# A two-layer diffusion trunk on one core: output groups over four PSUM banks, splits without GpSimd, and modulation groups and gating matmuls in other places

## The chip, the cores and the metric

The kernel runs on one core of a Trainium2 chip. The metric is the device time of one execution in microseconds; a lower time is better. Several executions are timed and the median is given, and one further execution is profiled. The engines are TensorE (PE: matmuls, with weight loads listed apart as PEld), VectorE (DVE), ScalarE (ACT), GpSimd (POOL) and the sync engine (SP), which here only issues transfers.

## The reference, cut to what matters

The program computes one inference step of a two-layer network for 512 latent tokens and 128 context tokens, 640 token columns in all, of width 1024. A conditioning vector (`c` for latent tokens, `c_ctx` for context tokens) gives nine modulation vectors for each layer, and each layer has a half-step feed-forward block, a mixer and a second half-step feed-forward block:

```
mod = (silu(cond) @ ada_w[i] + ada_b[i])                 # 9 vectors of 1024
h = modulate(rms_norm(x, g0), mod[0], mod[1]); x += 0.5 * mod[2] * swiglu(h)
h = modulate(rms_norm(x, g1), mod[3], mod[4]); x += mod[5] * mixer(h)
h = modulate(rms_norm(x, g2), mod[6], mod[7]); x += 0.5 * mod[8] * swiglu(h)
swiglu(h) = (silu(h @ w_g) * (h @ w_u)) @ w_out          # inner width 2816
```

The mixer of layer 0 has retention heads beside a spatial gating part (`u * (w_s @ rms_norm(v) + b_s)`), the mixer of layer 1 is differential attention. All values are fp32.

## The kernel before, in words

Activations lie with features on the 128 partitions and the 640 tokens along the free axis, in two halves of 320 columns. Each weight and each activation is split into a high part rounded to fp32r and a low part with the rest, and a product is three matmuls (high by high, high by low, low by high: lines 695, 696 and 697, in `mm3x`), here called a step. `tick()` after each step moves every waiting generator on by one.

**Weights and splits.** One list, `order`, holds every weight group and every modulation group in the order of use. The sync engine issues the loads in that order (`emit_load`, `pump`) into two raw buffers of 1 MB, the ring; a load waits until a buffer is released. `split_piece` makes the high part on ScalarE (line 308, tile `whi`) and the low part on VectorE (line 309, `wlo`), or on GpSimd where it is called so: twice before the first matmuls and twice for the second group of the first block.

**Feed-forward blocks.** Each of the four blocks has 22 inner groups of 128 features, in three stages of 6, 8 and 8. The first two groups go as a pair (in the very first block by `first_wide`), the third plainly, and the rest by a Strassen scheme (`strassen_in`) with seven products into three PSUM tiles `pu`, `pg`, `pf`. Its last VectorE and ScalarE instructions make the high and low part (`a...h`, `a...l`) of the group's activation. After each stage, `out_proj` multiplies the stage's 6 or 8 activations by four output groups `fout` of two column blocks each. For a column block and a half, `op_step` takes one PSUM bank, runs over all activations in order, and VectorE adds the result to the residual (`x_update`, tile `xs`).

**Modulation groups.** There are 36 for each layer. One kind (`ada`) runs on TensorE: 16 matmuls in a row, ahead of a feed-forward group; four such groups share a PSUM bank until the fourth is done. The other kind (`ada_v`, the set `ADV`) runs on VectorE: four passes over the raw buffer with a dot product against conditioning rows `sb`, which `load_condb` loads (1 MB) and ScalarE puts through SiLU. `mid_ada` starts such a group within an output stage as soon as the list comes to it. `weave` puts VectorE groups behind output groups and TensorE groups ahead of the feed-forward groups in `FA`.

**Order on the engines.** Most instructions are placed by a planner that works from its own estimates; `high_priority` moves a traced instruction ahead. SP is in written order throughout; TensorE, VectorE and ScalarE are in written order at the start, and TensorE through the Strassen groups and output stages. In the mixer of layer 0 the gating part (`sgu`) yields `SGW` ticks after its norm before its matmuls `mx` are issued.

Of the kernel before, what the change touches and what calls it, by code (L numbers as in the profile page):

```python
# [11 lines left out]
F32R = mybir.dt.float32r  # L12
I32 = mybir.dt.int32
AF = mybir.ActivationFunctionType
# [4 lines left out]
P = 128  # L19
# [15 lines left out]
NG0 = 3  # L35
FA = (4, 6, 9, 12, 14, 18)
QD_ = 512
# [3 lines left out]
NPRE = 10  # L41
SGW = 11
FYO = (0, 3, 4, 1, 5, 6, 2, 7)
# [16 lines left out]
C_N = 1280  # L60
ADV = {(0, g) for g in range(12, 36)} | {(1, g) for g in range(24)}
PHASES = ((0, 0), (0, 1), (0, 2), (1, 0), (1, 1), (1, 2))
# [5 lines left out]
def trunk_kernel(  # L68
# [153 lines left out]

    def weave(ws, ads, pads=(), fins=()):
        r, ads, pads = [], list(ads), list(pads)
        for w in ws:
            if pads and w[0] == "fin" and w[3] in fins:
                r.append(pads.pop(0))
            r.append(w)
            if ads and w[0] != "fin" and not (w[0] == "ein" and w[1] < 2):
                r.append(ads.pop(0))  # L230
        assert not ads and not pads
        return r
# [4 lines left out]
    order = order[:2] + w00[:1] + order[2:q] + w00[1:2] + order[q:]  # L237
    l1, pl = ada_groups(1, range(6)), ada_groups(1, range(6, 9))
    order += weave(w00[2:], ada_groups(0, [3, 4, 5]), ada_groups(0, [2]), (2, 3, 4, 5))
    order += weave([("ein", g) for g in range(10)] + [("eout", g) for g in range(4)], ada_groups(0, [6, 7, 8]))  # L240
    order += weave(ffn_order(0, 1), l1[:12], pl[:6], FA)
    order += weave(ffn_order(1, 0), l1[12:], pl[6:], FA)
    order += [("oin", g) for g in OORD] + [("oout", c, g) for c in range(2) for g in range(2)]
# [29 lines left out]

    def split_piece(sub=V):
        while st["sp"] < nord and order[st["sp"]][0] == "ada":
            st["sp"] += 1
        j = st["sp"]
        if j >= nord:
# [19 lines left out]
        else:  # L298
            nq = 1
            n = wtab[key][1] // 2 * 256  # L300
            t = r[:, h * n:(h + 1) * n]
        hi = wp.tile([P, 1024], F32R, tag="whi", bufs=5, name=f"whi{j}_{h}")
        lo = wp.tile([P, 1024], F32R, tag="wlo", bufs=5, name=f"wlo{j}_{h}")
        if key[0] == "fin":
            hf, lf = (v[:, :nq * QD_].rearrange("p (q x) -> p q x", q=nq) for v in (hi, lo))
        else:
            hf, lf = hi[:, :n], lo[:, :n]
        S.activation(out=hf, in_=t, func=AF.Copy)  # L308
        sub.tensor_tensor(out=lf, in0=t, in1=hf.bitcast(F32), op=ALU.subtract)  # L309
# [395 lines left out]
    def first_wide(i, keys, names):  # L705
# [13 lines left out]
        for c in SQ:  # L719
            if c in "ab":  # L720
                gs.append(ada(order[st["i"]]))
                next(gs[-1])
            elif c == "T":
                for g in gs:
                    next(g)
            elif c == "F":
                for g in gs:
                    for _ in g:
                        pass
                gs = []  # L730
                apply_all2((n, n + 1))
                n += 2
            elif c == "W":
                W1 = next_group(keys[1])
                split_piece(nc.gpsimd)
                split_piece(nc.gpsimd)
            elif c == "G":
                assert kg < n
                go(0, kg, W0, (0, 1))
                kg += 1  # L740
            elif c == "g":
                assert kw < n
                go(1, kw, W1, (0,))
                kw += 1
        assert kg == kw == KD
        load_condb()
        sg.__exit__(None, None, None)
# [63 lines left out]
    def out_proj(keys, acts, l, gmod, nxt, ks=None):  # L811
        nw = len(keys) if nxt is None else 2
        for gi in range(nw):
            W = next_group(keys[gi])
            for j in range(2):
                for hf in range(2):
                    op_step(keys[gi], W, gi, j, hf, acts, l, gmod, nxt, ks)
                    mid_ada()
            W.done()
# [5 lines left out]
        for n_, hf in enumerate((1, 0) if end else (0, 1)):  # L825
# [9 lines left out]
            chains[nxt, hf] = spawn(norm_chain(nxt, hf, NW[hf]))  # L835

    def op_step(key, W, gi, j, hf, acts, l, gmod, nxt, ks):
        ps = psm("op" + "_".join(str(v) for v in key[1:]) + f"_{j}{hf}")
        mm_fm(ps, W, j, acts, hf, ks)
        if nxt is None:  # L840
            x_update(ps, 2 * gi + j, l, gmod, hf)
        else:
            with tc.high_priority(HP):
                x_update(ps, 2 * gi + j, l, gmod, hf)
                norm_acc(nxt, hf, 2 * gi + j)

# [46 lines left out]
    def ffn(i, l, s, nxt):  # L893
        base = 0
        for ci, n in enumerate(CHUNKS):
# [35 lines left out]
            for g in range(g0, base + n):  # L931
                e = start_g(g)
                strassen_in(i, l, s, g, e)
                acts.append(e[:2])
            lastf = nxt if ci == len(CHUNKS) - 1 else None
# [587 lines left out]
    for _ in rsqrt(r, m, 5, "n0"):  # L1523
        pass
    split_piece(nc.gpsimd)
    split_piece(nc.gpsimd)
    warm(WU[2])
# [6 lines left out]
    for hf, (t0, t1) in enumerate(HALVES):  # L1534
        bc = psm(f"n0b{hf}")
        PE.matmul(bc[:, :t1 - t0], ones, dg[:, t0:t1], start=True, stop=True)
        t = stmp(f"bcs{hf}")
        S.copy(out=t[:, :t1 - t0], in_=bc[:, :t1 - t0])
        bcs[0, hf] = t
        prod[0, hf] = 0  # L1540
# [10 lines left out]

    apply_all2((0, 1))
    tb[0] = spawn(tbuild(0))
# [114 lines left out]
```

## Time and profile before

| what | value |
|---|---|
| median of the timed runs (lowest to highest) | 2477.71 us (2469.72 to 2481.81) |
| the profiled execution's own time | 2478.16 us |
| span of its profile | 2476.1 us |
| mean granted TensorE clock | 0.987 |
| TensorE busy | 2395.3 us (97%) |
| VectorE busy | 1840.8 us (74%) |
| ScalarE busy | 1067.4 us (43%) |
| GpSimd busy | 63.7 us (3%) |

The span runs from the first to the last instruction of the profiled execution. Busy time is the time in which an engine had an instruction in work; TensorE's instructions overlap and their ends are modelled, so its share says when it had work and not how fast it went. The granted clock is the share of full speed at which TensorE was let run.

### The profile page before, as it was taken

To read this page: it belongs to the slowest core of one execution; us is meant where nothing else is said; L and a number is where in the kernel's file an instruction comes from. 1 tells how busy PE (TensorE), PEld (TensorE's weight loads), DVE (VectorE), ACT (ScalarE), POOL (GpSimd) and SP (SyncE) were. 2 spreads that over 40 slices of the span, in tenths; PEclk is the share of its full clock that TensorE was granted. 3 is DMA by queue.
4 is the path that set the end of the run, shared out by engine and by line. 5 is a ranking of instruction groups with operands and counts; after the bars stand their busy time and mean duration, and the time that the engine had idled before them with its cause. 6 is when DMAs were issued, how large, how long until landed. Compare 5 with 4: busy or idle time off the path is not lost.

```text
span 2476.1 us, 40714 instructions
## 1 busy us (share of the span) xinstructions
PE 2395.3 (97%) x16530; PEld 2342.1 (95%) x16530; DVE 1840.8 (74%) x3749; ACT 1067.4 (43%) x2018; POOL 63.7 (3%) x86
## 2 busy tenths in 40 slices
PE   8999999999899999999999999999999999999998
PEld 6899999899899999999999999999999989999998
DVE  7677867877878777677977776789788878574664
ACT  4525335333226335153542423536777646252442
POOL 1000000000000000000000000001011000000000
PEclk8999999999999999999999999999999999999999
DMA  7342423323231433423234242242111111222121
GB/s 277 112 151 86 154 71 115 137 105 124 79 136 69 137 120 119 153 96 124 91 108 145 96 175 89 103 171 74 42 43 57 54 35 67 81 87 91 69 103 43
DMA packets 44476, 259.30 MB, mean 105 GB/s; under 512 B 5889, under 2 KB 8577, under 8 KB 16769
## 3 DMA queue, kind: packets, MB, share of 16 engines
q1 hardware_dynamic: 41024, 252.37, 28.6%
q8 instruction: 129, 2.11, 0.4%
q0 software_dynamic: 1280, 2.62, 0.3%
q10 hardware_dynamic: 1984, 1.72, 0.2%
q14 instruction: 59, 0.48, 0.1%
HBM read 252.76 MB, written 3.93 MB: 104 GB/s over the span
## 4 chain that ended last, share of the span: by engine, by line
PE 80%; DVE 9%; DMA 4%; ACT 4%; issue 2%; POOL 0%; POOLq 0%; ACTq 0%; DVEq 0%
PE op L696 8%; PE op L697 8%; PE op L695 8%; PE pu L695 6%; PE pu L696 6%; PE pu L697 6%; PE pg L697 3%; DVE wlo L309 3%; PE pg L696 3%; PE pg L695 3%; PE pf L695 3%; PE pf L696 3%; PE pf L697 3%; ACT whi L308 2%; DMA raw<-in_w_fout 2%
## 5 line engine op out<-in xcount | busy, mean ns | idle before, releaser
L309 DVE TENSOR_TENSOR wlo<-raw,whi 128x1024 fp32r<-128x1024 f32 (+1 forms) x480 | 528.8, 1118 | 286.0 <-ACT whi L308 284.9
L308 ACT ACTIVATE whi<-raw 128x1024 fp32r<-128x1024 f32 (+1 forms) x484 | 465.0, 976 | 639.7 <-DMA raw<-in_w_fout 144.1
L807 DVE SCALAR_TENSOR_TENSOR xs<-op,mod,xs 128x128 f32<-128x128 f32 (+2 forms) x312 | 126.9, 435 | 135.1 <-PE op L697 134.6
L524 ACT ACTIVATE nq<-xs 128x320 f32<-128x320 f32 x84 | 39.0, 468 | 135.1 <-DVE xs L807 133.3
L406 DVE CUSTOM_DVE_ANT_0 raw<-raw,sb 128x1024 f32<-128x1024 f32 x72 | 87.4, 1218 | 0.7
L404 DVE SCALAR_TENSOR_TENSOR raw<-raw,sb 128x1024 f32<-128x1024 f32 x72 | 87.5, 1220 | 0.5
L695 PE MATMUL oq<-H4h,whi 128*128 128x320 f32 x256 | 81.1, 318 | 0.2 <-ACT ov L979 0.2
L697 PE MATMUL oq<-H4h,wlo 128*128 128x320 f32 x256 | 79.6, 311 | 0.0
L696 PE MATMUL oq<-H4l,whi 128*128 128x320 f32 x256 | 79.3, 310 | 0.0
L1316 DVE TENSOR_REDUCE amx<-as 128x1 f32<-128x320 f32 x144 | 61.5, 460 | 19.1 <-PE as L1312 18.8
L1324 ACT ACTIVATE ap<-as,anm 128x320 f32<-128x320 f32 x128 | 66.2, 531 | 14.1 <-DVE anm L1319 13.9
L696 PE MATMUL pf<-H5p,whi 128*128 128x320 f32 x172 | 53.8, 313 | 2.0 <-DVE H5p L614 2.0
L871 ACT COPY p<-pg 128x320 f32<-128x320 f32 x76 | 32.5, 427 | 53.8 <-PE pg L697 53.6
L696 PE MATMUL pf<-H3p,whi 128*128 128x320 f32 x172 | 53.5, 312 | 1.8 <-DVE H3p L614 1.8
L696 PE MATMUL pf<-H2p,whi 128*128 128x320 f32 x172 | 53.4, 312 | 1.8 <-DVE H2p L614 1.8
L695 PE MATMUL pf<-H0p,whi 128*128 128x320 f32 x172 | 54.3, 318 | 0.2 <-ACT H0p L609 0.2
L696 PE MATMUL pf<-H0p,whi 128*128 128x320 f32 x172 | 53.9, 313 | 0.2 <-DVE H0p L614 0.2
L695 PE MATMUL pf<-H5p,whi 128*128 128x320 f32 x172 | 53.9, 317 | 0.0
L695 PE MATMUL pf<-H3p,whi 128*128 128x320 f32 x172 | 53.8, 317 | 0.0
L695 PE MATMUL pf<-H2p,whi 128*128 128x320 f32 x172 | 53.8, 316 | 0.0
L291 DVE TENSOR_TENSOR raw<-raw 128x512 f32<-128x512 f32 x76 | 52.4, 689 | 1.9
L697 PE MATMUL pf<-H0p,wlo 128*128 128x320 f32 x172 | 53.8, 313 | 0.0
(2691 smaller groups left out, 8835.6 us busy)
## 6 DMA issues: line engine op xcount, KB each, us to landing
raw<-in_w_fin SPq DMA_DIRECT2D x88, 1024.0 KB, 4.7
raw<-in_ada_w SPq DMA_DIRECT2D x64, 1024.0 KB, 4.8
raw<-in_w_fout SPq DMA_DIRECT2D x32, 1024.0 KB, 4.7
raw<-in_w_fout SPq DMA_DIRECT2D x16, 768.0 KB, 4.1
raw<-in_w_oin SPq DMA_DIRECT2D x12, 1024.0 KB, 4.8
raw<-in_w_ein SPq DMA_DIRECT2D x10, 1024.0 KB, 5.1
raw<-in_ada_w SPq DMA_DIRECT2D x32, 256.0 KB, 6.7
raw<-in_w_eout SPq DMA_DIRECT2D x4, 1024.0 KB, 6.2
```

The lines of the kernel that those rows point to most:

```text
L291: sub.tensor_tensor(out=a11, in0=a22, in1=a11, op=ALU.subtract)
L308: S.activation(out=hf, in_=t, func=AF.Copy)
L309: sub.tensor_tensor(out=lf, in0=t, in1=hf.bitcast(F32), op=ALU.subtract)
L404: V.scalar_tensor_tensor(out=o, in0=w, scalar=1.0, in1=sb[:, c * D:(c + 1) * D], op0=ALU.mult, op1=ALU.mult, accum_out=r)
L406: V.tensor_tensor_reduce(out=o, in0=w, in1=sb[:, c * D:(c + 1) * D], scale=1.0, scalar=0.0, op0=ALU.mult, op1=ALU.add, accum_out=r)
L524: S.activation(out=q[:, :n], in_=x[k][:, t0:t1], func=AF.Square)
L695: PE.matmul(o, wh, xh, start=start, stop=False, skip_group_check=more)
L696: PE.matmul(o, wh, xl, start=False, stop=False, skip_group_check=more)
L697: PE.matmul(o, wl, xh, start=False, stop=stop, skip_group_check=more)
L807: V.scalar_tensor_tensor(out=x[m][:, a:b], in0=ps[:, a - t0:b - t0], scalar=mod[:, l, gmod * KD + m, c:c + 1], in1=x[m][:, a:b], op0=ALU.m ...
L1316: V.tensor_reduce(out=mx[:, j, a:a + 1], in_=sps[j][a][:, 0:w], axis=AX.X, op=ALU.max, negate=True)
L1324: S.activation(out=pj[j][:, a * 320:a * 320 + w], in_=sps[j][a][:, 0:w], func=AF.Exp, bias=b, accum_out=(sm[:, j, a:a + 1] if full else s2 ...
```

## The change

Output groups: the first output group of each feed-forward stage goes through a new function `op_wide`. It opens four PSUM banks, one for each column block and half, and runs over all activations but the last two in each of them, then over the last but one in each, then over the last in each; `mid_ada` is called once, after the second of these cuts.

Modulation groups: the four groups of layer 1's third modulation vector (groups 8 to 11) move from VectorE to TensorE, so that 44 groups and not 48 go on VectorE. `FA` has eight places in each of two blocks, not six, and no longer the one ahead of feed-forward group 6. Behind the fourth output group of these blocks' first stage no VectorE group stands any more.

Start: the subtractions of the first four weight pieces are on VectorE, not on GpSimd. The first high part is made early, by `split_hi`, and the first low part is made between the two halves of the first activation.

Conditioning rows: `load_condb` is called after the Strassen group 4 of the first block, not at the end of `first_wide`. Gating matmuls: `SGW` is 30, not 11.

```diff
-FA = (4, 6, 9, 12, 14, 18)
+FA = (4, 8, 10, 12, 15, 16, 18, 20)
-SGW = 11
+SGW = 30
-ADV = {(0, g) for g in range(12, 36)} | {(1, g) for g in range(24)}
+ADV = {(0, g) for g in range(12, 36)} | {(1, g) for g in range(24) if g // 4 != 2}
...
-            if ads and w[0] != "fin" and not (w[0] == "ein" and w[1] < 2):
+            if ads and w[0] != "fin" and not (w[0] == "ein" and w[1] < 2) and w[3:] not in skip:
                 r.append(ads.pop(0))
...
-    l1, pl = ada_groups(1, range(6)), ada_groups(1, range(6, 9))
+    l1, pl = ada_groups(1, (0, 1, 3, 4, 5)), ada_groups(1, (2, 6, 7, 8))
...
-    order += weave(ffn_order(0, 1), l1[:12], pl[:6], FA)
-    order += weave(ffn_order(1, 0), l1[12:], pl[6:], FA)
+    order += weave(ffn_order(0, 1), l1[:11], pl[:8], FA, ((0, 3),))
+    order += weave(ffn_order(1, 0), l1[11:], pl[8:], FA, ((0, 3),))
...
+    def split_hi(j, h):
+        hi = pre[j, h] = wp.tile([P, 1024], F32R, tag="whi", bufs=5, name=f"whi{j}_{h}")
+        t = raw[j].rearrange("p (m h x) -> p h m x", m=2, h=2)[:, h]
+        S.activation(out=hi.rearrange("p (m x) -> p m x", m=2), in_=t, func=AF.Copy)
...
             elif c == "W":
                 W1 = next_group(keys[1])
-                split_piece(nc.gpsimd)
-                split_piece(nc.gpsimd)
+                split_piece()
+                split_piece()
...
         assert kg == kw == KD
-        load_condb()
         sg.__exit__(None, None, None)
...
             W = next_group(keys[gi])
+            if gi == 0 and keys[0][0] == "fout":
+                op_wide(keys[0], W, acts, l, gmod, nxt)
+                continue
             for j in range(2):
...
+    def op_wide(key, W, acts, l, gmod, nxt):
+        n = len(acts)
+        cuts = ((0, n - 2), (n - 2, n - 1), (n - 1, n))
+        jh = [(j, hf) for j in range(2) for hf in range(2)]
+        ps = {}
+        for c, (a, b) in enumerate(cuts):
+            for j, hf in jh:
+                if c == 0:
+                    ps[j, hf] = psm("op" + "_".join(str(v) for v in key[1:]) + f"_{j}{hf}")
+                for k in range(a, b):
+                    mm3(ps[j, hf], W, j, k, acts[k], hf, k == 0, k == n - 1)
+                if c == 2:
+                    op_end(ps[j, hf], j, hf, l, gmod, nxt)
+            if c == 1:
+                mid_ada()
+        W.done()
...
                 strassen_in(i, l, s, g, e)
+                if i == 0 and g == 4:
+                    load_condb()
                 acts.append(e[:2])
...
-    split_piece(nc.gpsimd)
-    split_piece(nc.gpsimd)
+    skip_raw()
+    split_hi(st["sp"], 0)
     warm(WU[2])
...
-        S.copy(out=t[:, :t1 - t0], in_=bc[:, :t1 - t0])
+        with tc.high_priority(HP):
+            S.copy(out=t[:, :t1 - t0], in_=bc[:, :t1 - t0])
...
-    apply_all2((0, 1))
+    with tc.high_priority(HP):
+        norm_apply(0, 0, 0)()
+        split_piece()
+        norm_apply(0, 1, 0)()
+    apply_all2((1,))
+    split_piece()
     tb[0] = spawn(tbuild(0))
```

The evacuation that `op_step` and `op_wide` share is now `op_end` (the residual update, and the norm's sum where a norm follows), and `split_piece` takes a high part that is there already.

## Rows read from the trace of the kernel before

**Rows 1.** The page, parts 1 and 4: TensorE's busy time, share of the span and instructions (PEld, DVE, ACT and POOL behind it), and the chain of work that ended last, its share of the span by engine.

```profile
PE 2395.3 (97%) x16530; PEld 2342.1 (95%) x16530; DVE 1840.8 (74%) x3749; ACT 1067.4 (43%) x2018; POOL 63.7 (3%) x86
...
PE 80%; DVE 9%; DMA 4%; ACT 4%; issue 2%; POOL 0%; POOLq 0%; ACTq 0%; DVEq 0%
```

**Rows 2.** TensorE's waits over the whole span: the line and tile that waited and whom it waited for, us in total, times, the longest.

```profile
PE mx L1186 <- DVE evs L1005: 7.5, 1, 7.5
PE pg L695 <- ACT whi L308: 5.4, 2, 2.8
...
PE adaps L447 <- ACT a000s L905: 2.8, 1, 2.8
...
PE pg L697 <- DVE wlo L309: 2.5, 3, 1.1
PE op L695 <- ACT whi L308: 2.5, 2, 2.0
...
PE op L696 <- DVE a1021l L891: 1.1, 1, 1.1
...
PE op L696 <- DVE a115l L891: 0.2, 1, 0.2
```

**Rows 3.** The timeline of TensorE at the start of the second output stage of the first block: start and duration in us, then the instruction, and in brackets the idle time before it and what ended it.

```profile
276.27 0.31 PE L695 MATMUL op<-a0012h,whi 128*128 128x320 f32 x1
...
276.71 0.31 PE L695 MATMUL op<-a0013h,whi 128*128 128x320 f32 x1
278.06 0.42 PE L696 MATMUL op<-a0013l,whi 128*128 128x320 f32 x1 [1.04 <-DVE a0013l L891]
```

**Rows 4.** The sync engine's timeline in the second block, between its first output stage and feed-forward group 6 (two loads in one line), and two pieces of the chain of work there (start, us, what).

```profile
862.47 1.47 SPq L264 DMA_DIRECT2D raw<-in_ada_w  x2
...
872.41 1.13 DVE raw L406
873.58 4.72 DMA raw<-in_w_fin
```

**Rows 5.** Busy time of the engines in four stretches (us from the span's start): the stretch and its length, then PE, PEld, DVE, ACT and POOL with their instructions, the granted clock, the DMA share and GB/s.

```profile
755.00:767.00 12.00, 10.70 (x73) 10.27 (x71) 9.83 (x44) 5.72 (x16) 0.00 (x0) 1.00 0.01 4
...
632.00:635.00 3.00, 2.80 (x12) 2.83 (x13) 2.54 (x15) 0.00 (x0) 0.00 (x0) 0.50 0.65 270
887.66:891.08 3.42, 3.42 (x15) 3.42 (x14) 1.23 (x1) 1.23 (x2) 0.00 (x0) 0.50 0.69 220
612.00:650.00 38.00, 30.53 (x214) 28.65 (x213) 34.81 (x110) 9.00 (x15) 1.09 (x2) 0.91 0.24 87
```

**Rows 6.** The timeline of TensorE within the third of these stretches: two matmuls one behind the other.

```profile
888.73 0.47 PE L696 MATMUL pu<-T20bl,whi 128*128 128x320 f32 x1
889.00 0.47 PE L697 MATMUL pu<-T20bh,wlo 128*128 128x320 f32 x1
```

**Rows 7.** VectorE's work behind the gating matmuls, 612 to 643 us, grouped by line: instructions, then busy us, mean ns of one, idle us before.

```profile
L1190 DVE TENSOR_TENSOR mt<-mx,bt 128x512 f32<-128x512 f32 (+1 forms) x4 | 1.9, 486 | 0.3 <-PE mx L1186 0.3
L1194 DVE TENSOR_TENSOR mt<-mt,gu 128x640 f32<-128x640 f32 x2 | 1.6, 820 | 0.0
...
L509 DVE TENSOR_TENSOR sgo1l<-mt,sgo1h 128x640 fp32r<-128x640 f32 x1 | 0.8, 824 | 0.0
```

**Rows 8.** The timelines of VectorE and, in the lowest row, of GpSimd in the first 60 us.

```profile
23.09 1.09 DVE L469 TENSOR_TENSOR mod<-adar,adab 128x4 f32<-128x4 f32 x1
24.22 2.28 DVE L425 SCALAR_TENSOR_TENSOR coefA<-mod,ng 128x4 f32<-128x4 f32 x1
...
26.71 0.55 DVE L607 SCALAR_TENSOR_TENSOR H0t<-xs,coefA,bcs 128x320 f32<-128x320 f32 x1
...
46.14 0.94 DVE L585 TENSOR_TENSOR H0t<-H0t 128x320 f32<-128x320 f32 x1 [1.96 <-ACT H0t L582]
47.18 2.44 DVE L586 TENSOR_TENSOR H0t<-H0t,H0t 128x320 f32<-128x320 f32 x1
49.66 0.49 DVE L587 TENSOR_TENSOR H0t<-H0t,H0t 128x320 f32<-128x320 f32 x1
...
56.51 2.35 DVE L309 TENSOR_TENSOR wlo<-raw,whi 128x1024 fp32r<-128x1024 f32 x2
...
21.82 4.66 POOL L309 TENSOR_TENSOR wlo<-raw,whi 128x1024 fp32r<-128x1024 f32 x2 [21.36 <-ACT whi L308]
```

**Rows 9.** ScalarE's timeline: the copies of the broadcast norm factor (two in one line), and the SiLU over the conditioning rows.

```profile
24.50 0.97 ACT L1538 COPY bcs<-n0b 128x320 f32<-128x320 f32 x2 [1.81 <-PE n0b L1536]
...
71.15 1.89 ACT L188 ACTIVATE sb<-sb 128x2048 f32<-128x2048 f32 x1
```

**Rows 10.** TensorE's timeline: the matmuls of one modulation group.

```profile
102.24 1.07 PE L447 MATMUL adaps<-raw,sc 128*32 128x256 f32 x16
```

**Rows 11.** The first output stage of the first block, in timelines: TensorE's first matmul, VectorE's first pass of the first and of the second modulation group, the sync engine's load of output group 2, and VectorE's first low part of it.

```profile
130.79 0.31 PE L695 MATMUL op<-a000h,whi 128*128 128x320 f32 x1
...
134.83 1.22 DVE L404 SCALAR_TENSOR_TENSOR adaj<-raw,sb 128x1024 bf16<-128x1024 f32 x1
...
137.58 1.23 DVE L404 SCALAR_TENSOR_TENSOR adaj<-raw,sb 128x1024 bf16<-128x1024 f32 x1
...
142.86 0.33 SPq L267 DMA_DIRECT2D raw<-in_w_fout  x1
...
147.91 0.96 DVE L309 TENSOR_TENSOR wlo<-raw,whi 128x768 fp32r<-128x768 f32 x1 [1.24 <-ACT whi L308]
```

More of the change, by code (lines that the diff above doesn't have):

```diff
@@ L221, in ffn_order, with weave @@
         return r
-    def weave(ws, ads, pads=(), fins=()):
+    def weave(ws, ads, pads=(), fins=(), skip=()):
         r, ads, pads = [], list(ads), list(pads)
@@ L272, in pump, with skip_raw, split_piece @@
             emit_load()
-    def split_piece(sub=V):
+    def skip_raw():
         while st["sp"] < nord and order[st["sp"]][0] == "ada":
             st["sp"] += 1
+    pre = {}
+    def split_hi(j, h):
+        hi = pre[j, h] = wp.tile([P, 1024], F32R, tag="whi", bufs=5, name=f"whi{j}_{h}")
+        t = raw[j].rearrange("p (m h x) -> p h m x", m=2, h=2)[:, h]
+        S.activation(out=hi.rearrange("p (m x) -> p m x", m=2), in_=t, func=AF.Copy)
+    def split_piece(sub=V):
+        skip_raw()
         j = st["sp"]
@@ L301, in split_piece @@
             t = r[:, h * n:(h + 1) * n]
-        hi = wp.tile([P, 1024], F32R, tag="whi", bufs=5, name=f"whi{j}_{h}")
+        early = pre.pop((j, h), None)
+        hi = early or wp.tile([P, 1024], F32R, tag="whi", bufs=5, name=f"whi{j}_{h}")
         lo = wp.tile([P, 1024], F32R, tag="wlo", bufs=5, name=f"wlo{j}_{h}")
@@ L307, in split_piece @@
             hf, lf = hi[:, :n], lo[:, :n]
-        S.activation(out=hf, in_=t, func=AF.Copy)
+        if early is None:
+            S.activation(out=hf, in_=t, func=AF.Copy)
         sub.tensor_tensor(out=lf, in0=t, in1=hf.bitcast(F32), op=ALU.subtract)
@@ L839, in op_step, with op_end @@
         mm_fm(ps, W, j, acts, hf, ks)
+        op_end(ps, 2 * gi + j, hf, l, gmod, nxt)
+    def op_end(ps, m, hf, l, gmod, nxt):
         if nxt is None:
-            x_update(ps, 2 * gi + j, l, gmod, hf)
+            x_update(ps, m, l, gmod, hf)
         else:
             with tc.high_priority(HP):
-                x_update(ps, 2 * gi + j, l, gmod, hf)
-                norm_acc(nxt, hf, 2 * gi + j)
+                x_update(ps, m, l, gmod, hf)
+                norm_acc(nxt, hf, m)
     def strassen_in(i, l, s, g, e):
@@ L1524, in trunk_kernel @@
         pass
-    split_piece(nc.gpsimd)
-    split_piece(nc.gpsimd)
+    skip_raw()
+    split_hi(st["sp"], 0)
     warm(WU[2])
```

## The prediction

> **What bounds the kernel now.** I read the page first. TensorE is busy for 97% of the span and holds 80% of the chain that ended last, VectorE 9% [rows 1]. So the kernel is one list of matmuls issued in order, and a change pays only where it fills a gap of TensorE, and costs only what it adds to TensorE. The second view is the list of TensorE's waits [rows 2]. It is short, and most of it is a few places: the gating matmuls `mx` (7.5 us, once), the first products of a Strassen group (`pg`, 5.4 us in two and 2.5 us in three waits), modulation matmuls near the start (2.8 us), and thirteen waits of an output group `op` for the newest activation, `a...h` or `a...l` (10.9 us in all; the first and the last of the thirteen are shown, each is 1.1 us at most). The third view is TensorE's timeline at such a place [rows 3]. The matmul that waits starts 1.35 us after the one before; the three before it, which wait for nothing, take 0.44 us from start to start, 0.147 each, so it lost 1.20 us where the list says 1.0. The list counts from a modelled end, and I add 0.16 us to each of its waits. The fourth view is the granted clock. After a long wait it stands at 0.50, the lower of its two levels (1.2 instead of 2.4 GHz), for a while [rows 5], and there the same matmuls start 0.267 us apart [rows 6], so 45% of such a stretch is lost. A long wait costs more than its own length.
>
> **Part by part.**
>
> *Output group over four banks.* A step is three matmuls, 0.44 us. Before, the first chain of steps (one bank, all activations) needs the newest activation after 5 or 7 steps, 2.2 or 3.1 us; now it is needed after 20 or 28 steps, 8.8 or 12.3 us, so the thirteen waits go: 10.9 + 13 x 0.16 = 13.0 us. The number of matmuls is the same. Four banks at once, the three of the last Strassen group and the one that a modulation row may hold make eight, which is all there are, so I see no wait for a bank; the four evacuations come closer together, but the next chain needs none of their banks. Gain 13.0 (bounds 10 and 13.5).
>
> *Modulation groups moved.* Four groups of layer 1 go from VectorE to TensorE. One such group takes TensorE 1.07 us [rows 10], so 4.3 us are lost for certain. VectorE is freed of 16 passes of 1.22 us [rows 11], 19.5 us that stand beside TensorE's work and give nothing directly. The transfers are the same 1 MB loads in another order, and there lies the gain. Before, a VectorE group and a TensorE group stood between the last output weights and feed-forward group 6, in two of the four feed-forward blocks. The sync engine issued both loads at 862.5, and that of group 6 only at 873.58, when VectorE's last pass over the first (from 872.41) had released a buffer, to land 4.7 us later [rows 4]. That is the first of the two long `pg` waits. Now neither stands between, and the load can go at 862.5, 11 us sooner, more than the wait. Of [rows 2] go the 5.4 us and, of the 2.5 us, the 1.4 us that follow in the same two groups, plus 4 x 0.16: 7.4 us. With the waits go two stretches of lower clock, 45% of 3.42 us each [rows 5]: 3.1 us. Gain 10.5 (bounds 7 and 10.5).
>
> *Gating matmuls later.* 19 more steps of 0.44 us are 8.4 us, more than the 7.5 us waited. But VectorE is busy for 34.8 of the 38 us around this place [rows 5]: it is late, and `mx` is where TensorE meets that lateness. If `mx` moves back, the next product that needs VectorE waits instead. What helps is that VectorE's own work behind `mx` for groups 0 and 1 moves back with it: 1.9 + 1.6 + 2 x 0.8 = 5.1 us [rows 7]. I take 5.1 us, and 1.3 us for the lower clock that follows, 45% of the some 2.9 us up to 635 [rows 5]. Gain 6.4 (bounds 0, if VectorE fills the room with other work, and 7.7 + 1.3 = 9.0).
>
> *No GpSimd in the first splits.* While GpSimd works on its pair of subtractions (4.66 us, and a like pair from 44.3), VectorE's instructions stretch: `mod` 1.09 and `coefA` 2.28 us, `H0t` 0.94 and 2.44 us, against 0.49 us for the next of its kind [rows 8]. If the small ones shrink to some 0.2 us, 3.0 us go there, and 2.4 us at 46 to 50. Of the 3.0 only 1.7 count, since `H0t` at 26.71 then waits for the broadcast copy, whose first half ends at 25.0 [rows 9]. Added on VectorE are four subtractions, 2.35 us a pair [rows 8]; the 1.96 us of idle time before 46.14 can hide most of the second pair. Net 1.7 + 2.4 - 2.35 - 0.4 = +1.4, or -0.6 if nothing hides, and ScalarE's steps ahead of a subtraction add latency. I take 0 (bounds -2 and +2).
>
> *Conditioning rows later.* ScalarE's SiLU over these rows, 1.89 us [rows 9], stands right ahead of the evacuation `a000s` that modulation matmuls wait for (2.8 us, rows 2): 1.9 us gained. At its new place the transfer goes on the sync queue behind group 5's load and ahead of the first output load; it waits for no buffer, so nothing behind it is held, and its first reader comes only at 134.83 [rows 11]. There the 1.89 us on ScalarE may push back a weight copy: bounds 0 and 1.9.
>
> *A wait that the change adds.* The first VectorE modulation group of an output stage is now issued after 20 steps, not after 6 steps and the 1.8 us of two waits: 8.8 - 4.4 = 4.4 us later, unless the planner fetches it forward. Behind it on the sync queue stands the load of output group 2, which goes when VectorE's passes over the buffer are done. Before: issue at 142.86, first low part done at 148.87 [rows 11], 6.0 us. Now 147.3 + 6.0 = 153.3, and TensorE, which starts the stage at 130.79 [rows 11], needs it 48 steps and two matmuls later, at 152.2: 1.1 us of wait in each of three stages of six activations, 3.3 us. The stages of eight have 64 steps (28 us), which is enough, but for the last of the first block, whose late weights already cost an `op` a 2.0 us wait for `whi` [rows 2]; 7.6 us more delay there could cost up to 5.7. Bounds 0 and 9.0. I take 2.0, nearer to 0, since the planner does fetch forward: the second modulation group of the first stage began at 137.58 [rows 11], while its place is 30 steps and the waits behind 130.79, at 145.8.
>
> *Sum.* 13.0 + 10.5 + 6.4 + 0 + 1.9 - 4.3 - 2.0 = 25.5 us off the profiled execution of 2478.2 us (span 2476.1 and 2.1 around it): 2452.7. That execution is 0.5 us above the median of the three runs, which lie within 12 us of each other, so 2453 stands for the median.
>
> **The rivals.**
>
> *Lateness handed on.* The waits were only the shallow spots of a pipeline that VectorE and the two weight buffers pace: `mx` passes its wait on (6.4 us lost), and the modulation group behind the wide order costs 9.0 and not 2.0. For it: VectorE's 92% around `mx`. Against it: between its passes VectorE has room in the output stages. 2452.7 + 6.4 + 7.0 = 2466, still lower than before, by a little less than 0.5%.
>
> *The change doesn't bring group 6 forward.* If both weight buffers stay taken while output group 3 is split, the `pg` waits stay: 2452.7 + 10.5 = 2463. Against it: one buffer is freed of its modulation row for certain.
>
> *Slower: the rotation breaks TensorE's stream.* If stepping over four banks left TensorE short of work between steps and its clock fell in the twelve wide groups, each stretch of 3.42 us at the lower level would cost 1.5 us. Three in each group are 36 x 1.5 = 54 us: 2507. The change loses from 17 stretches (25.5 / 1.5) on. Against it: from 755 to 767 the first pair of a block steps over four banks in the same way, and the clock stands at 1.00 [rows 5]. The Trainium skill (TensorE: Matmul & The Clock Gate, section "A second HAM failure mode: psum-queue depth-cycling") tells of a kernel that lost throughput to just this, short idle times between groups when it cycled its banks; by that rule this change would lose, and this kernel's trace does not agree with it.
>
> **How the numbers follow.** The sum with its terms inside their bounds: 0.66. Lateness handed on: 0.17. Group 6 not early: 0.10. Rotation: 0.04. The last 0.03 are a planned order that comes out slower at a place I can't name. With all terms at their best the gain is 13.5 + 10.5 + 9.0 + 2 + 1.9 - 4.3 = 32.6, 2446, and 4 us of spread between runs make the low end 2442; the high end, 2471, is the first rival with that spread. Some 12.4 us (0.5%) is about what a measurement of this kernel can tell from no change. The sum is faster but for a small tail, group 6 not early (15 us gained) mostly, lateness handed on (12 us) about half the time: 0.76 faster, 0.18 the same, and with the rotation and the unnamed place 0.06 slower.
>
> **What would show it.** Right: no `op` wait for an `a...h` or `a...l` tile in the list; the `pg` waits at group 6 gone and the clock at 1.00 behind them; four more runs of 16 modulation matmuls; no subtraction on GpSimd; the SiLU over the rows near 115 us. Wrong: an `op` waiting for `whi` at the third output group of the stages of six; an `sp` or `up` matmul waiting for VectorE soon after 630 for about as long as `mx` did; a granted clock under 1 inside an output stage.

## The result

The changed kernel takes 2453.72 us (median of four runs, 2448.58 to 2457.18), the kernel before 2478.43 us beside it. The ratio is 0.9903 with a 95% interval of 0.9886 to 0.9920, so it is faster by 24 us, between 20 and 28. Forecast were 2453 us and a gain of 25.5 us; the profiled span went from 2476.1 to 2453.1 us. The total came out as forecast, but three of its terms were mis-sized and one part was worth less alone than in company; the errors cancelled.

### The profile page after: what moved, and what is told of

The parts are those of the page before. It is cut to its first block, busy times and chain, and to the rows that moved or that the text cites. A ratio compares the mean times of both kernels' runs of the same rounds, so it can differ in the third digit from the quotient of the medians.

```text
span 2453.1 us, 40798 instructions
## 1 busy us (share of the span) xinstructions
PE 2391.2 (97%) x16596; PEld 2337.1 (95%) x16596; DVE 1818.8 (74%) x3723; ACT 1065.3 (43%) x2018; POOL 53.0 (2%) x82
## 4 chain that ended last, share of the span: by engine, by line
PE 80%; DVE 10%; DMA 4%; ACT 3%; issue 1%; POOL 0%; POOLq 0%; ACTq 0%; DVEq 0%
PE op L707 8%; PE op L708 8%; PE op L709 8%; PE pu L707 7%; PE pu L709 6%; PE pu L708 6%; PE pf L707 3%; PE pf L708 3%; PE pg L709 3%; PE pf L709 3%; PE pg L707 3%; PE pg L708 3%; DVE wlo L321 3%; DMA raw<-in_w_fin 3%; ACT whi L320 2%
## 5 line engine op out<-in xcount | busy, mean ns | idle before, releaser
L320 ACT ACTIVATE whi<-raw 128x1024 fp32r<-128x1024 f32 (+2 forms) x483 | 462.4, 975 | 612.2 <-PE op L708 137.9
L418 DVE CUSTOM_DVE_ANT_0 raw<-raw,sb 128x1024 f32<-128x1024 f32 x60 | 72.9, 1220 | 0.7
L1360 ACT ACTIVATE ap<-as,anm 128x320 f32<-128x320 f32 x128 | 66.2, 531 | 14.1 <-DVE anm L1355 13.9
L709 PE MATMUL pf<-H3p,wlo 128*128 128x320 f32 x172 | 54.2, 316 | 0.0
L707 PE MATMUL pf<-H0p,whi 128*128 128x320 f32 x172 | 53.6, 314 | 0.0
L709 PE MATMUL pf<-H5p,wlo 128*128 128x320 f32 x172 | 53.4, 312 | 0.0
```

Of the source, the lines that this page charges most:

```text
L418: V.tensor_tensor_reduce(out=o, in0=w, in1=sb[:, c * D:(c + 1) * D], scale=1.0, scalar=0.0, op0=ALU.mult, op1=ALU.add, accum_out=r)
L707: PE.matmul(o, wh, xh, start=start, stop=False, skip_group_check=more)
L709: PE.matmul(o, wl, xh, start=False, stop=stop, skip_group_check=more)
L1360: S.activation(out=pj[j][:, a * 320:a * 320 + w], in_=sps[j][a][:, 0:w], func=AF.Exp, bias=b, accum_out=(sm[:, j, a:a + 1] if full else s2 ...
```

## The profile after

The page, part 1, against [rows 1]: 66 more matmuls, and 10.7 us less on GpSimd.

```profile
PE 2391.2 (97%) x16596; PEld 2337.1 (95%) x16596; DVE 1818.8 (74%) x3723; ACT 1065.3 (43%) x2018; POOL 53.0 (2%) x82
```

TensorE's waits over the span, columns as in [rows 2]:

```profile
PE pg L709 <- DVE wlo L321: 3.7, 4, 1.2
...
PE op L707 <- ACT whi L320: 3.1, 1, 3.1
...
PE adaps L459 <- ACT a000s L939: 2.6, 1, 2.6
...
PE pg L707 <- ACT whi L320: 1.5, 1, 1.5
PE op L709 <- DVE wlo L321: 1.5, 3, 0.7
...
PE pu L707 <- ACT a005s L908: 1.0, 1, 1.0
```

Against [rows 2], `mx` is gone, no `op` waits for an `a...h` or `a...l` tile any more, and `pg` waits for `whi` once, not twice. The `op` waits for late weights (`whi`, `wlo`) and the `pg` waits for `wlo` are longer than before, the wait for `a000s` is 2.6 us where it was 2.8, and one for `a005s` is new. All waits of this list together went from 73.0 to 54.2 us.

The granted clock, in stretches that answer those of [rows 5] (columns as there): three output stages, and the stretch of the gating matmuls.

```profile
130.00:160.00 30.00, 30.00 (x206) 30.00 (x206) 24.80 (x48) 3.16 (x4) 0.00 (x0) 1.00 0.44 162
270.00:300.00 30.00, 30.00 (x206) 30.00 (x205) 25.62 (x44) 7.13 (x8) 0.00 (x0) 1.00 0.43 152
...
1130.00:1160.00 30.00, 30.00 (x207) 30.00 (x206) 22.68 (x42) 8.16 (x14) 0.00 (x0) 1.00 0.36 128
...
612.00:650.00 38.00, 38.00 (x269) 35.19 (x268) 33.14 (x110) 11.81 (x25) 1.09 (x2) 1.00 0.25 88
```

In each of the twelve wide groups TensorE steps over four banks without idle time, and the clock stands at 1.00. The time at the lower level fell from 65.0 to 46.4 us over the whole execution.

Where the gain arose is told by the start of the same matmul in the two traces (us):

| stretch of work up to ... | start before | start after | change in the stretch |
|---|---|---|---|
| first output stage | 130.79 | 127.76 | -3.0 |
| its end | 174.81 | 169.85 | -1.9 |
| second output stage (groups 6 to 13) | 273.63 | 271.26 | +2.6 |
| its end | 331.10 | 327.43 | -1.3 |
| last step of the first block | 493.94 | 492.18 | +1.9 |
| end of the mixer | 736.72 | 723.22 | -11.7 |
| second block's first output stage, its end | 879.43 | 865.30 | -0.6 |
| within its group 6 | 889.00 | 869.26 | -5.6 |
| its second stage, end | 1044.90 | 1024.28 | -0.9 |
| its last output stage (groups 14 to 21) | 1146.13 | 1130.51 | +5.0 |
| third block's first output stage, its end | 1337.19 | 1320.56 | -1.0 |
| within its group 6 | 1347.37 | 1324.52 | -6.2 |
| its second stage, end | 1503.35 | 1481.07 | +0.6 |
| its last output stage (groups 14 to 21) | 1604.65 | 1587.14 | +4.8 |
| last matmuls of the fourth block | 2461.98 | 2439.04 | -5.4 |

The large gains stand where they were forecast: at the gating matmuls and at group 6 of two blocks. Only the 5.4 us of the last stretch are more than the two `op` waits there were worth (1.6 us). The three losses of 2.6, 5.0 and 4.8 us had no place in the forecast but for the four added modulation groups (two in each of the last two, some 2.1 us each).

## The experiments

Ratios are to the kernel before, run on the same chip, with 95% intervals; positions come from one profiled execution of each kernel.

### Parts of the change alone

**The wide output group alone**, `op_wide` and `op_end` as in the change, nothing else:

```diff
+            if gi == 0 and keys[0][0] == "fout":
+                op_wide(keys[0], W, acts, l, gmod, nxt)
+                continue
```

> The kernel before with the output group over four banks alone. Both theories: the thirteen op waits for a...h and a...l tiles go, 13.0 us by the rows of before. Theory A (a gain is only kept where the weight loads keep up): the VectorE modulation group of the stage starts later, as in the trace after, so some of it comes back at the next feed-forward group. In the trace after 2.5 us came back at group 6 of the first block and about 2 us in that block's last output stage; here the group-6 waits of the second and third block (2.76 + 0.86 and 2.92 + 0.86 us) would also grow by some 1.5 us each. Sum 13.0 - 2.5 - 2 - 3 = 5.5 us faster, ratio 0.998. Theory B (the waits were independent of each other): 13.0 us faster, ratio 0.995, and the group-6 waits are no longer than before. If the rotation hurt TensorE the granted clock would fall in the twelve groups and the time would be above that of before.

2469.11 us, ratio 0.9965 (0.9953 to 0.9978): 8.7 us faster, between 5.4 and 11.6. The thirteen waits are gone. TensorE's waits near group 6 of the second block (860 to 900 us) and of the third (1320 to 1345 us), in this kernel:

```profile
PE pg L695 <- ACT whi L308: 2.2, 1, 2.2
PE pu L695 <- ACT whi L308: 1.5, 1, 1.5
PE pg L697 <- DVE wlo L309: 0.7, 1, 0.7
PE pu L697 <- DVE wlo L309: 0.7, 1, 0.7
...
PE pu L695 <- ACT whi L308: 1.8, 1, 1.8
PE pg L695 <- ACT whi L308: 1.5, 1, 1.5
PE pu L697 <- DVE wlo L309: 0.6, 1, 0.6
PE pg L697 <- DVE wlo L309: 0.4, 1, 0.4
```

That is 5.1 and 4.3 us, where the kernel before waited 3.3 and 3.5. At group 6 of the first block 2.2 us stand where there was nothing. So some 5 us of new waits stand a few groups later: the weights there come when the weight buffers and VectorE let them, and a TensorE that arrives earlier waits for them. By positions, with the lower clock behind these waits, more comes back: the three stretches of the table that hold group 6 are 4.1, 3.1 and 3.3 us longer than in the kernel before, while the mixer (2.3 us) and the start (1.6 us) are shorter here, which the edit doesn't touch. Theory A, not B.

**Gating matmuls alone**: `SGW = 30`.

> The kernel before with the gating matmuls 30 and not 11 ticks behind their norm, and nothing else. Theory A (VectorE late at one place with idle time behind it): the mx wait of 7.6 us and the 1.5 us of lower clock behind it go and nothing takes their place, 9.1 us faster, ratio 0.9963, with the granted clock at 1.00 from 600 to 660. My prediction's own value: 6.4 us, as 2.5 us of the wait come back. Rival (lateness handed on): an sp, up or eg matmul waits for VectorE for about 7 us instead, no gain, ratio 1.000.

2466.53 us, ratio 0.9957 (0.9944 to 0.9970): 10.7 us faster, between 7.4 and 13.9. The stretch of [rows 5] in this kernel:

```profile
612.00:650.00 38.00, 38.00 (x268) 35.19 (x267) 33.25 (x112) 11.46 (x24) 1.08 (x2) 1.00 0.25 87
```

TensorE is busy for all 38 us and VectorE for 33.25. The whole wait went and nothing took its place: from 480 to 720 us TensorE's list of waits is empty, so the small waits of the kernel before at the mixer's first input groups, at a norm and at an output group are gone here too. The stretch from the first block's last step to the end of the mixer is 11.8 us shorter, as in the changed kernel (11.7). My 6.4 us lie below the interval.

**Modulation groups alone**: `FA`, `ADV`, `skip` and the two `weave` calls of layer 1.

> The kernel before with the modulation groups moved alone (four groups to TensorE, their eight places ahead of feed-forward groups, no VectorE group behind output group 3 in the second and third block). Theory A, from the trace after: the group-6 waits of these two blocks and the lower clock behind them go (10.8 us), four more runs of 16 matmuls cost 4.3 us, and the eight places ahead of groups bring new waits for weights in the stages of groups 14 to 21, some 4 us in the two blocks: 10.8 - 4.3 - 4 = 2.5 us faster, ratio 0.999. My prediction: no such waits, 10.5 - 4.3 = 6.2 us faster, ratio 0.9975. Rival: group 6 isn't brought forward, 4.3 us slower, ratio 1.0017.

2476.52 us, ratio 0.9995 (0.9983 to 1.0006): 1.2 us faster, between 4.2 faster and 1.5 slower. My 6.2 us are excluded, theory A's 2.5 are not, and 4.3 us slower are excluded too. The waits at group 6 of the two blocks are gone. But a `pg` waits for `wlo` at 1077 and at 1532 us, 1.05 us each from start to start, where none did before. One wait grew in a stage that this edit doesn't touch, the second of the first block: `op` waits 2.0 us for `a0013h`, and the stretch is 3.9 us longer. There ScalarE makes the same instructions in the same order as before, but the weight copies ahead of `a0013h` wait for a load:

```profile
275.97 2.00 ACT L308 ACTIVATE whi<-raw 128x1024 fp32r<-128x1024 f32 x2 [3.02 <-DMA raw<-in_w_fout]
```

That load was issued at 268.86 us, as before (269.05), but took 7.0 us to land and not 4.7. The same load took 6.5 us in the changed kernel and 4.8 in the run with 14 for 15 below, and these two kernels are alike up to there, so its time differs between executions. I put the wait down to the profiled execution, which at 2479.4 us was one of the slower ones of its kernel, and not to the edit.

**The start alone**: `split_hi` early, the subtractions on VectorE, the first between the two halves, the copies of the broadcast norm factor moved ahead.

> The kernel before with the start of the change alone (no GpSimd subtractions, first high part early, first low part between the activation's halves); the conditioning rows stay where they were. My prediction: 0, between 2 us faster and 2 slower. Theory A, from the trace after: VectorE's small instructions no longer stretch and TensorE's wait of 4.7 us at 51 shrinks, so that the T00 tiles are 3.3 us earlier; the clock also doesn't fall behind that wait. 3.3 us faster at the first group of Strassen products, and kept to the end: ratio 0.9987. The position of the matmul at 73.42 in the trace before tells it: 70.1 by theory A, 73.4 by the prediction.

2477.03 us, ratio 1.0003 (0.9993 to 1.0012). TensorE's timeline in this kernel at the matmul that waits for `a000s`, and at a later wait; then the first of these matmuls in the kernel with the wide group alone, whose start is that of the kernel before:

```profile
70.30 0.42 PE L459 MATMUL adaps<-raw,sc 128*32 128x256 f32 x4 [1.78 <-ACT a000s L917]
...
103.62 0.41 PE L709 MATMUL pg<-T00ah,wlo 128*128 128x320 f32 x1 [0.81 <-DVE wlo L321]
```

```profile
71.75 0.42 PE L447 MATMUL adaps<-raw,sc 128*32 128x256 f32 x4 [2.77 <-ACT a000s L928]
```

The kernel before had 73.42 in its own profile, but 71.6 to 72.0 in the three runs above that leave its start alone: executions of one start differ by 1.9 us, and the profiled one was a late one. Against 71.75 the new start is 1.4 us earlier, and a new wait of 0.81 us at 103.62 takes most of that back: at 118.8 both kernels are level. So the start is worth nothing measurable by itself, as forecast, and theory A took 1.9 us of an unlucky execution for a gain.

**The wide group and the modulation groups together**, the edits of the first and third run:

> The kernel before with two parts of the change, the output group over four banks and the moved modulation groups. Alone they gave ratios of 0.9965 and 0.9995. If they don't touch each other, 8.6 + 1.2 = 9.8 us faster, ratio 0.996. Theory A: alone, the wide group gave 3.5 us back at group 6 of the second and third block, where the waits grew from 7.4 to 10.9 us; with the modulation groups gone from there none of these waits is left, so the two together give 9.8 + 3.5 = 13.3 us, ratio 0.9946, and no pu or pg wait near group 6 of these two blocks. Rival: the wide order's late start of VectorE's passes still makes group 6 late, by 1 to 3 us in each block.

2464.52 us, ratio 0.9946 (0.9934 to 0.9958): 13.4 us. Between 860 and 900 us, and between 1310 and 1350, the list of waits is empty. That theory is what the traces show: the two stretches up to within group 6 are 5.6 and 6.2 us shorter than before, just as with the moved groups alone, where the wide group alone made them 3.1 and 3.3 us longer. What it gave back there is kept once no modulation group stands ahead of it. The times alone don't decide it, since the sum of 9.8 us lies within the noise of the three runs.

### Parts undone or moved in the changed kernel

**Conditioning rows back** at the end of `first_wide`:

```diff
+        load_condb()
         sg.__exit__(None, None, None)
...
-                if i == 0 and g == 4:
-                    load_condb()
```

> The changed kernel with the conditioning rows loaded where they were before, at the end of the first pair, and nothing else undone. My prediction: 1.9 us slower than the changed kernel, since ScalarE's SiLU of 1.89 us again stands ahead of the evacuation a000s. Theory A adds what the trace after shows at the new place: there the SiLU (119.37) stands ahead of a weight copy and the evacuation a005s, and TensorE waits 1.2 us at 122.38; that wait goes here. Position of the matmul at 68.44 in the trace after: 70.3 by both; at the first output stage the loss is 0.7 us by theory A and 1.9 by the prediction. The total, 0.7 to 1.9 us, is too small for the timing (ratio to before 0.9905 where the changed kernel gave 0.9903); the traces decide. Rival: the wait at 68.44 (2.7 us) doesn't change, as TensorE came as much earlier as the evacuation did; then 0.

2455.62 us, ratio 0.9912 (0.9897 to 0.9927), not to be told from the changed kernel by the time. The same matmul in this kernel, and in the changed one, which also has a wait that this one lacks:

```profile
70.34 0.42 PE L459 MATMUL adaps<-raw,sc 128*32 128x256 f32 x4 [1.75 <-ACT a000s L940]
```

```profile
68.44 0.42 PE L459 MATMUL adaps<-raw,sc 128*32 128x256 f32 x4 [2.63 <-ACT a000s L939]
...
122.38 0.41 PE L707 MATMUL pu<-T00ah,whi 128*128 128x320 f32 x1 [1.04 <-ACT a005s L908]
```

It comes 1.9 us later, the length of the SiLU, though the wait is shorter: TensorE came 2.8 us later as well. The cause is the clock. Around the same two waits (0.67 and 1.94 us, at 45 to 48 us) it stood at 0.51 here and at 1.00 in the changed kernel, and 23 matmuls were run where the other ran 42 (columns as in [rows 5], this kernel first):

```profile
46.90:53.80 6.90, 5.91 (x23) 5.92 (x24) 6.68 (x16) 5.90 (x11) 0.00 (x0) 0.51 0.67 283
```

```profile
46.90:53.80 6.90, 6.03 (x42) 6.04 (x43) 6.71 (x15) 5.78 (x11) 0.00 (x0) 1.00 0.32 133
```

The time lost so cost nothing, as the matmul waits for ScalarE in both. The rival that reads the length of the wait alone is wrong. At group 6 (175.01 against 173.39) 1.6 us are left: the SiLU's new place costs the 1.04 us at 122.38, and its old place a wait of 0.8 at 103.66, which the run of the start alone shows too.

**VectorE's group earlier within the wide group:**

```diff
-            if c == 1:
-                mid_ada()
+                if c == 0 and (j, hf) == (0, 1):
+                    mid_ada()
```

> The changed kernel with the stage's first VectorE modulation group started after the second chain of the wide output group (8 or 12 steps) and not after its second cut (20 or 28 steps). Theory A (the wide order's late call holds the buffer, and so the loads behind it): the pg waits at group 6 of the first block (1.63 + 0.86 us) and the whi and wlo waits of that block's last output stage (3.29 + 0.86 + 0.67 + 0.41, and 1.5 for the lower clock behind) go, some 7 us faster than the changed kernel, ratio to before 0.9875. Rival: VectorE's passes of 1.22 us now stand ahead of the newest activation's low part, and op waits for a...l come back in nine stages, up to 1.2 us each: no gain or up to 4 us slower, ratio 0.9903 to 0.992.

2453.23 us, ratio 0.9902 (0.9887 to 0.9917), not to be told from the changed kernel. SP's loads in the first block's last output stage (of a modulation group or an output group, in turn), in the changed kernel and in this one, and VectorE's first and last pass over the first of these modulation groups in the changed kernel:

```profile
429.97 0.33 SPq L264 DMA_DIRECT2D raw<-in_ada_w  x1
451.71 0.33 SPq L267 DMA_DIRECT2D raw<-in_w_fout  x1
456.99 0.33 SPq L264 DMA_DIRECT2D raw<-in_ada_w  x1
459.96 0.33 SPq L267 DMA_DIRECT2D raw<-in_w_fout  x1
...
442.01 1.22 DVE L416 SCALAR_TENSOR_TENSOR adaj<-raw,sb 128x1024 bf16<-128x1024 f32 x1
...
450.46 1.21 DVE L416 SCALAR_TENSOR_TENSOR raw<-raw,sb 128x1024 f32<-128x1024 f32 x1
```

```profile
435.55 0.33 SPq L267 DMA_DIRECT2D raw<-in_w_fout  x1
443.93 0.33 SPq L264 DMA_DIRECT2D raw<-in_ada_w  x1
457.13 0.33 SPq L267 DMA_DIRECT2D raw<-in_w_fout  x1
```

The load of output group 2 goes 16 us earlier, as theory A says. But that of output group 3, behind the next modulation group, goes only 2.8 us earlier, and now TensorE waits for its weights: 2.4 us in two waits, where 4.6 stood in four. This stage is 3.1 us shorter than in the changed kernel, just what it had lost there; the profiled spans differ by 2.0 us, and the medians by less than their noise. At group 6 of the first block nothing changed (idle 1.50 and 0.70 us, 1.47 and 0.70 in the changed kernel): the stage's first pass begins at 130.7 here and at 130.8 there, so the planner had fetched it forward before. So the late call holds output group 2 of the last stage, but is not the cause of the wait at group 6, and on VectorE one lateness passes to the next load.

**No two neighbours in `FA`**: `(4, 8, 10, 12, 14, 16, 18, 20)`, 14 for 15.

> The changed kernel with the TensorE modulation group that stands ahead of feed-forward group 15 put ahead of group 14 in both blocks, so that no two neighbouring groups have one. Theory A (two loads in a row between the weights of neighbouring groups make group 16 late): the pg waits at 1055.74 and 1512.12 (1.05 and 1.04 us) and the smaller ones around them (0.40, 0.51, 0.46, 0.32) go, 2 to 4 us faster than the changed kernel, ratio to before 0.989. Rival: the load ahead of group 14 stands behind a VectorE group again, as the one ahead of group 6 did before, and a pg wait of 2.5 to 3 us comes at group 14 in both blocks, with the lower clock behind it: 3 to 5 us slower, ratio 0.992.

2448.44 us, ratio 0.9884 (0.9867 to 0.9900), against 0.9903 of the changed kernel; the intervals overlap, the traces are plain. TensorE's waits from 1020 to 1075 us in the changed kernel:

```profile
PE pg L709 <- DVE wlo L321: 0.9, 1, 0.9
PE pu L707 <- DVE p L915: 0.3, 1, 0.3
PE pu L707 <- ACT a0114s L908: 0.2, 1, 0.2
```

Here this list is empty, and that from 1470 to 1530 too. The two stretches of groups 14 to 21 cost 3.7 and 3.1 us more than before, not 5.0 and 4.8; 2.1 of each are the two added modulation groups. With the edit before it added:

> The changed kernel with both edits, the earlier VectorE group in the wide output group and the place ahead of group 14 in the stead of 15. Theory A: the two gains add, 9 to 11 us faster than the changed kernel, ratio to before 0.9862. Rivals as for the two edits alone: no gain, ratio 0.990, or slower, 0.993.

2450.98 us, ratio 0.9896 (0.9881 to 0.9911). The two gains do not add: in the trace the first block's last output stage is 3.4 us shorter than with the 14 alone, and the mixer behind it 2.4 us longer.

**No VectorE group ahead of group 6 in the first block**, on top of the 14:

```diff
-    order += weave(w00[2:], ada_groups(0, [3, 4, 5]), ada_groups(0, [2]), (2, 3, 4, 5))
+    l0 = ada_groups(0, [3, 4, 5, 6, 7, 8])
+    order += weave(w00[2:], l0[:11], ada_groups(0, [2]), (2, 3, 4, 5), ((0, 3),))
...
-            if ads and w[0] != "fin" and not (w[0] == "ein" and w[1] < 2) and w[3:] not in skip:
+            if ads and w[0] != "fin" and not (w[0] == "ein" and w[1] < 1) and w[3:] not in skip:
...
-    order += weave([("ein", g) for g in range(10)] + [("eout", g) for g in range(4)], ada_groups(0, [6, 7, 8]))
+    order += weave([("ein", g) for g in range(10)] + [("eout", g) for g in range(4)], l0[11:])
```

> The changed kernel with the place ahead of group 14 in the stead of 15, and in the first block too no VectorE modulation group behind output group 3 of the first stage: layer 0's groups each move one place back, the last of the first block goes behind the second input group of the mixer. Theory A (that group's passes and its buffer make group 6 late): the pg waits of 2.3 + 0.86 us at 173 go, and the lower clock behind them where it falls, 3 to 5 us faster than with the place ahead of group 14 alone (2448.4), ratio to before 0.987. Rival (lateness handed on): the wait shows up at the input groups of the mixer, whose second one now has a VectorE group behind it, 1 to 3 us at an eq or ek matmul: 2447 to 2450, ratio 0.988 to 0.989.

2446.46 us, ratio 0.9864 (0.9845 to 0.9883), against 0.9884 with the 14 alone; these intervals overlap too. In the changed kernel, and then in this one, the first products of group 6:

```profile
173.39 0.42 PE L707 MATMUL pg<-T00ah,whi 128*128 128x320 f32 x1 [1.47 <-ACT whi L320]
173.65 0.31 PE L708 MATMUL pg<-T00al,whi 128*128 128x320 f32 x1
174.65 0.42 PE L709 MATMUL pg<-T00ah,wlo 128*128 128x320 f32 x1 [0.70 <-DVE wlo L321]
```

```profile
171.28 0.31 PE L708 MATMUL pg<-T00ah,whi 128*128 128x320 f32 x1
171.43 0.31 PE L709 MATMUL pg<-T00al,whi 128*128 128x320 f32 x1
171.57 0.31 PE L710 MATMUL pg<-T00ah,wlo 128*128 128x320 f32 x1
```

No wait, and none at the mixer's input groups in exchange. In all three blocks the wait at group 6 goes with the modulation group that stands ahead of it. In the first block it takes the wide group too: without that, in the kernel before, TensorE came later and found the weights ready.

**Nor one behind output group 0 of the last stage**: `skip` is `((0, 3), (2, 0))`, the cut of `l0` is at 10, and `w[1] < 0`.

> As the run before it, and also no VectorE group behind output group 0 of the first block's last stage, so that the mixer's first input group has one behind it too. Theory A: the load of that stage's output group 2 no longer waits for VectorE's passes, and the whi and wlo waits of 3.2 + 0.7 us at 459 go with the lower clock behind them: 4 to 5 us faster than the run before it, ratio to before 0.9855. Rival: these passes are then done beside the mixer's normalization and first input groups, where VectorE is the late one, and waits for eq, ek or n11 matmuls take as much: no gain on the run before it, ratio 0.987 to 0.989.

2444.00 us, ratio 0.9856 (0.9833 to 0.9878), the lowest of all: 36 us below the kernel before, some 10 below the changed one, but not to be told from the run before it. The waits from 430 to 510 us, without and with this edit:

```profile
PE op L708 <- ACT whi L321: 3.2, 1, 3.2
PE n10b L568 <- DVE n10d L565: 1.6, 1, 1.6
PE op L710 <- DVE wlo L322: 0.7, 1, 0.7
```

```profile
PE op L710 <- DVE wlo L322: 1.4, 2, 0.7
PE n10b L568 <- DVE n10d L565: 1.1, 1, 1.1
PE eq L709 <- DVE H1l L627: 1.0, 2, 0.6
PE n11p L556 <- DVE nq L541: 0.7, 1, 0.7
PE n11b L568 <- DVE n11d L565: 0.3, 1, 0.3
```

Of the 3.9 us at the weights 1.4 are left, and 2.0 us at the mixer's norm and first inputs come in: theory A's place with much of the rival's price.

## Why the prediction was right or wrong

**Output group, -13.0.** Right on the waits and on the clock of the wide groups. Wrong was to cost the step for itself: alone it gave 8.7 us, since its gain runs into late weights at the next group 6. In the change as a whole no such waits come at group 6 of the second and third block, where the modulation groups went; in the first 2.6 us came back. That is the first rival, lateness handed on, in a part of its size and at a place that I had not named.

**Modulation groups, -10.5 and +4.3.** Group 6 came forward as worked out from [rows 4]: the two stretches gained 5.6 and 6.2 us, of which 1.07 each is a modulation group that stands elsewhere now. The step that failed is the cost of the new places. I priced them by TensorE's 1.07 us [rows 10] and not by the load that each puts between two weights, though the part opens with just that mechanism for group 6. The two stretches of groups 14 to 21 lost 9.8 us and not the 4.3 of four groups; with 14 for 15 they lost 6.8. Alone, the part gave 1.2 us (at most 4.2), not 6.2.

**Gating matmuls, -6.4.** The mechanism was right, a term too small. I counted only VectorE's work that moves back and let the rest of the wait return, for VectorE is at 92% around it [rows 5]. But it is late with the one result that `mx` reads: with `SGW` at 30 alone, TensorE waits for nothing from 480 to 720. The full 7.6 us and the 1.3 us of lower clock behind went, 8.9 us.

**Start, 0, and conditioning rows, -1.9.** Both held: no measurable gain by the start alone, and 1.6 us left of the moved rows by the first output stage. VectorE's small instructions shrank as read from [rows 8]: `mod` to 0.17, `coefA` to 0.16 us.

**The added wait, +2.0.** The mechanism was right, the place partly wrong. At output group 2 of the stages of six there is no wait: in the first of them the planner fetched the first pass forward, to 3.1 us behind the stage's start (4.0 before), and the load went at 137.43, sooner than before. In the first block's last stage, which I named, the late passes hold output group 2's load until 451.71 (441.02 before), and the stretch loses 1.9 us where it should have gained 1.3; with the call made earlier these 3.1 us came back. I count here the 2.6 us at group 6 too, which no other term holds, though the earlier call left them as they were: 5.8, within my bounds of 0 and 9.0.

**Rotation.** Refuted: the clock stands at 1.00 in the wide groups, as it did in the pair of [rows 5]. The rule of the Trainium skill that I set against the change (TensorE: Matmul & The Clock Gate, section "A second HAM failure mode: psum-queue depth-cycling") tells of short idle times between groups of matmuls; here the groups over four banks leave none, and by this trace stepping over banks is no loss in itself.

So the total fits by cancelling, and that it fits within 2 us is luck. The added wait took 3.8 us more than I priced and the new places 5.5 (9.8 - 4.3); the gating matmuls gave 2.5 more (8.9 - 6.4), the mixer's other waits 2.8 (11.7 - 8.9), and the start 1.1 (3.0 - 1.9), most of it the late start of the execution profiled before. 25.5 - 3.8 - 5.5 + 2.5 + 2.8 + 1.1 is 22.6, where the span fell by 23.0. The mixer's small waits are gone in the run of the gating matmuls alone as well; why, no run shows.

Smaller things cancel too. The stretches up to 879.43 and 1337.19 held op waits worth 1.8 and 3.1 us, but gained 0.6 and 1.0: after a norm the clock stayed at its lower level for 3.4 us longer in each. The last stretch, with op waits of 1.6 us, gained 5.4: there the lower level lasted 3.4 us less (1.5 us of work) and a norm's wait of 1.2 us is gone. None of these was forecast.

## What to carry to other kernels

A wait removed is worth its length only if the loads behind it can come earlier too: look for the next place where TensorE meets a load, and change both together. A group that is put ahead of other work costs the load that it puts in the queue, not only its own time; two in a row cost more than two apart (here 5.5 and 2.5 us beyond the matmuls, over two blocks). An engine at 92% need not be the bound: ask which of its results is needed first, and whether the reader has other work to do meanwhile.

## What was not expected of the hardware

The clock's fall behind a short wait comes and goes. In the run of the start alone it stood at 0.76 in the 6.8 us behind the `op` waits at 837 us (1.1 and 0.4 us), in the kernel before at 1.00 behind the same waits (1.0 and 0.4 us):

```profile
838.90:845.70 6.80, 6.80 (x38) 6.80 (x37) 6.74 (x14) 0.00 (x0) 0.00 (x0) 0.76 0.17 70
```

```profile
840.60:847.40 6.80, 6.80 (x48) 6.80 (x48) 6.80 (x16) 0.00 (x0) 0.00 (x0) 1.00 0.14 59
```

In the same 6.8 us 38 matmuls were run and not 48, which is 1.4 us of work. The runs of the gating matmuls alone and of the modulation groups alone show the same two waits, and the fall behind them. One profiled execution can't tell such a wait's full price: the start differs by 1.9 us between the profiles of kernels that share it, and one and the same load of 1 MB took between 4.6 and 7.3 us to land in eight profiles.
